# Four-layer decoder trunk on one core: sums of scaled x made in two parts and placed between the plain column tiles of each FFN

## The chip, the cores and the metric

The kernel runs on one core of a Trainium2 chip. The core's engines run side by side, each in the order of its own list of instructions, and wait for each other through semaphores: PE (TensorE) multiplies matrices, DVE (VectorE) and ACT (ScalarE) work element by element, POOL (GpSimd) and SP (SyncE) here mostly start transfers. The metric is device time in microseconds (us) of one execution; three runs of the kernel before took 1972.0 to 1973.74 us, median 1972.96 us. The profile is of a fourth execution.

## The reference, cut to what matters

Two layers; each is FFN, mixer, FFN. The mixer of layer 0 is differential attention, that of layer 1 a gated spatial MLP. x is 512 tokens by 1024 features in float32, an FFN's inner width is 2816.

```python
def _rmsnorm(x, g):
    y = xf * lax.rsqrt(jnp.mean(xf * xf, axis=-1, keepdims=True) + RMS_EPS)
    return (y * g.astype(jnp.float32)).astype(x.dtype)

def _swiglu_ffn(x, w_gate_up, w_down):
    g, u = jnp.split(x @ w_gate_up, 2, axis=-1)
    return (jax.nn.silu(g) * u) @ w_down

for i in range(DEPTH):
    x = x + 0.5 * _swiglu_ffn(_rmsnorm(x, ffn1_norm[i]), ffn1_w_gate_up[i], ffn1_w_down[i])
    # mixer: x = x + attention(_rmsnorm(x)) in layer 0, x + sgu(_rmsnorm(x)) in layer 1
    x = x + 0.5 * _swiglu_ffn(_rmsnorm(x, ffn2_norm[i]), ffn2_w_gate_up[i], ffn2_w_down[i])
```

## The kernel before, in words

**Layout.** x lies transposed in SBUF, eight tiles x[k] of 128 features by 512 tokens. Each fp32 operand of a product is split into a high part in a reduced format and the low rest (`hi`, `lo`; ACT copies the high part, DVE subtracts), and a product is three matmuls, hi·hi, hi·lo and lo·hi (`mm3`). So each weight piece of 128 by 1024 costs ACT a copy (`...h`) and DVE a subtraction (`...l`) before PE can use it (`split`, buffers in a ring of four).

**The four FFNs** are named f0 to f3 (f0 and f1 stand around the attention, f2 and f3 around the MLP; their norms are n0, n2, n3, n5). The 22 column tiles of gate and up form eleven pairs (j, j + 11). The first two pairs are made plainly: four *plain tiles*, 0, 11, 1, 12 in this order, of 48 matmuls 128x512 each: eight k, gate and up, three matmuls. Their weight pieces are called f1w{tile}{half}: f1w110 is the first half of tile 11, f1w11 the second half of tile 1. The other nine pairs are made in seven products instead of eight (names P1, P2, Q3, Q4, Q5, P6, P7), each for gate (a) and up (b): 14 *turns* of 12 matmuls 128x256, in the order P1a, P1b, Q5a, P6a, P6b, Q5b, P7a, P7b and so on. These products need sums and differences of weight pieces and seven *sums of scaled x* per kp = 0..3 (x[kp] and x[kp + 4] times the norm's gain and the row scale, with their halves added and subtracted). After the third, sixth and ninth pair, and at the end, `down_part` does a part of the down projection.

**The row scale.** The plain products use x times the gain only; the row scale 1/rms is multiplied in later. PE sums the squares (`Norm.rstd`, tile n2ss in f1), DVE makes the reciprocal root in some ten small steps (n2v, n2y, n2t), builds two diagonal tiles (n2dgh, n2dgl), PE spreads them over the partitions (`Norm.rows`, n2rb), ACT copies the result (n2rbs, `rb` in the code). In every FFN before, the sum of squares stands in the PE's list after k = 3 of a plain tile (the second tile in f0, the first in the others), the spreading after k = 7 of that tile.

**What `rb` lets go.** `gated` makes silu(gate)·up of a plain tile, `halves_of` splits it for the down projection, `scaled(kp)` makes the seven sums of one kp in one tile and splits them at once (f1x0h, f1x0l: 128x1792). In the program, `scaled` for all four kp is written after all four plain tiles, and P1a of the first pair (w2, tile f1w2Xa) needs all four.

**Order.** PE's order inside an FFN is the program's (`keep_in_program_order`). The lists of DVE and ACT are made by the tile framework's scheduler, which may move an instruction past others; once compiled the order is fixed.

Of the kernel before, what the change touches and what calls it, by code (L numbers as in the profile page):

```python
# [56 lines left out]
def kernel(  # L57
# [220 lines left out]
    def ffn(layer, which, norm, nxt):  # L278
# [10 lines left out]
        slot = {"P1": 0, "P2": 1, "Q4": 2, "Q5": 3, "P6": 4, "P7": 5, "Q3": 6}  # L289
        turns = ["P1a", "P1b", "Q5a", "P6a", "P6b", "Q5b", "P7a", "P7b", "P2a", "P2b", "Q3a", "Q3b", "Q4a", "Q4b"]  # L290

        with ExitStack() as c:
# [17 lines left out]
            xf, rb, late = [], None, []  # L310

            def gated(j, ps):
                h = room(f"{nm}r{j}")
                g, u = h[:, :2, :], h[:, 2:4, :]
# [4 lines left out]
                late_halves.append((j, u))  # L319

            def scaled(kp):

                h = room(f"{nm}x{kp}")
                for k, dst in ((kp, h[:, 0:8:7, :]), (kp + 4, h[:, 1:3, :])):
# [12 lines left out]
                xf.append((hi, lo))  # L337

            late_halves = []
            plain = [j for i in range(PLAIN) for j in (i, i + FH)]  # L340
            held = []
            for at, j in enumerate(plain):
                if first and at == 0:
                    parts = begin(norm)
                else:
                    parts = [
                        split(load(gate_up[f, j][:, q * D:(q + 1) * D], f"{nm}gu{j}{q}"), D, f"{nm}w{j}{q}")
                        for q in range(2)
                    ]
                ps = [bank(f"{nm}p{j}{u}", "ps" if first and at == 1 else "pp") for u in range(2)]  # L350
                for k in range(KT):
                    wh, wl = parts[k // 4]
                    for u in range(2):
                        c0 = slice((k % 4 * 2 + u) * P, (k % 4 * 2 + u + 1) * P)
# [1 line left out]
                    if rb is None and at == first:
                        if k == 3:
                            r = norm.rstd()
                        elif k == KT - 1:
                            rb = norm.rows(r)  # L360
                late.append((j, ps))
                if at == 1:
                    for unit in late:
                        gated(*unit)
                    late = []
            for kp in range(4):
                scaled(kp)
            for unit in late:
                gated(*unit)
            for unit in late_halves:  # L370
                halves_of(*unit)

            def gate_up_pair(i):
# [653 lines left out]
```

## Time and profile before

The profiled execution took 1971.33 us; its span, first to last instruction, is 1969.6 us.

| | busy us | share of the span | instructions |
|---|---|---|---|
| PE | 1935.8 | 98% | 11626 |
| PEld (weight loads of PE) | 1712.2 | 87% | 11626 |
| DVE | 1327.3 | 67% | 2127 |
| ACT | 879.0 | 45% | 1336 |
| POOL | 65.1 | 3% | 83 |

The mean granted clock of TensorE over the span is 0.992 of full speed. The chain that ended last is 92% PE, 6% DVE, 1% ACT and 1% issue. A share of busy time is a mean over the whole program; a busy matmul at half the clock counts as busy too. So the places where PE waits, and what it does right behind them, have to be read from the timeline.

### The profile page before, as it was taken

To read this page: it belongs to the slowest core of one execution; us is meant where nothing else is said; L and a number is where in the kernel's file an instruction comes from. 1 tells how busy PE (TensorE), PEld (TensorE's weight loads), DVE (VectorE), ACT (ScalarE), POOL (GpSimd) and SP (SyncE) were. 2 spreads that over 40 slices of the span, in tenths; PEclk is the share of its full clock that TensorE was granted. 3 is DMA by queue.
4 is the path that set the end of the run, shared out by engine and by line. 5 is a ranking of instruction groups with operands and counts; after the bars stand their busy time and mean duration, and the time that the engine had idled before them with its cause. 6 is when DMAs were issued, how large, how long until landed. Compare 5 with 4: busy or idle time off the path is not lost.

```text
span 1969.6 us, 29451 instructions
## 1 busy us (share of the span) xinstructions
PE 1935.8 (98%) x11626; PEld 1712.2 (87%) x11626; DVE 1327.3 (67%) x2127; ACT 879.0 (45%) x1336; POOL 65.1 (3%) x83
## 2 busy tenths in 40 slices
PE   8899999999999999999999999999999999999999
PEld 7889898877777799999879999988888887999997
DVE  8757574667878866666686666755595568666663
ACT  5535353555654444445445344533332234444451
POOL 0000000000000000000000000000000000000000
PEclk9899999999999999999999999999999999999999
DMA  6354552312112345454335546443333233454542
GB/s 206 97 141 133 140 136 89 129 64 70 55 54 86 83 131 148 131 140 131 112 82 137 130 138 150 124 140 116 105 116 97 86 107 86 133 144 132 139 124 80
DMA packets 89275, 228.58 MB, mean 116 GB/s; under 512 B 10033, under 2 KB 43185, under 8 KB 89137
## 3 DMA queue, kind: packets, MB, share of 16 engines
q1 hardware_dynamic: 78768, 188.95, 29.5%
q0 software_dynamic: 10368, 37.75, 11.5%
q8 instruction: 91, 1.49, 0.3%
q14 instruction: 48, 0.39, 0.1%
HBM read 224.56 MB, written 2.10 MB: 115 GB/s over the span
## 4 chain that ended last, share of the span: by engine, by line
PE 92%; DVE 6%; issue 1%; ACT 1%; DMA 0%; SPq 0%
PE f3dp L133 6%; PE f0dp L133 6%; PE f2dp L133 6%; PE f1dp L133 6%; PE gup L133 4%; PE gop L133 4%; PE aop L133 2%; PE v1p L133 1%; PE qk2p L133 1%; PE v0p L133 1%; PE qk1p L133 1%; PE qk0p L133 1%; PE gv0p L133 1%; PE gv1p L133 1%; PE gv2p L133 1%; PE gv3p L133 1%
## 5 line engine op out<-in xcount | busy, mean ns | idle before, releaser
L439 DVE SCALAR_TENSOR_TENSOR x<-f3dp,x 128x512 f32<-128x512 f32 x32 | 22.1, 691 | 60.2 <-PE f3dp L133 60.2
L439 DVE SCALAR_TENSOR_TENSOR x<-f0dp,x 128x512 f32<-128x512 f32 x32 | 22.1, 690 | 49.1 <-PE f0dp L133 49.1
L439 DVE SCALAR_TENSOR_TENSOR x<-f2dp,x 128x512 f32<-128x512 f32 x32 | 22.1, 690 | 49.1 <-PE f2dp L133 49.1
L439 DVE SCALAR_TENSOR_TENSOR x<-f1dp,x 128x512 f32<-128x512 f32 x32 | 22.1, 690 | 48.9 <-PE f1dp L133 48.9
L918 DVE TENSOR_TENSOR x<-gop,x 128x512 f32<-128x512 f32 x24 | 16.6, 690 | 20.0 <-PE gop L133 20.0
L898 ACT ACTIVATE gh<-gut 128x512 fp32r<-128x512 f32 x16 | 10.1, 633 | 42.6 <-DVE gut L897 42.6
L761 DVE TENSOR_TENSOR x<-aop,x 128x512 f32<-128x512 f32 x32 | 21.5, 685 | 1.9 <-PE aop L133 1.8
L888 PEld LDWEIGHTS gs<-wT,gv 128*128 128x128 f32 x128 | 16.1, 191 | 0.9
L893 DVE TENSOR_TENSOR gst<-gs,bs 128x512 f32<-128x512 f32 x16 | 11.0, 687 | 8.8 <-PE gs L888 8.8
L888 PE MATMUL gs<-wT,gv 128*128 128x128 f32 x128 | 16.2, 274 | 0.0
L838 ACT ACTIVATE gv<-gv 128x512 f32<-128x512 f32 x16 | 10.1, 629 | 12.4 <-DVE gv L837 12.3
L857 DVE TENSOR_TENSOR gut<-gup,n4rbs 128x512 f32<-128x512 f32 x16 | 10.9, 684 | 6.6 <-PE gup L133 6.6
L858 ACT ACTIVATE gut<-gut,sm 128x512 f32<-128x512 f32 x16 | 11.5, 721 | 6.7 <-DVE gut L857 6.5
L899 DVE TENSOR_TENSOR gl<-gut,gh 128x512 fp32r<-128x512 f32 x16 | 11.0, 686 | 4.2 <-ACT gh L898 4.2
L264 POOL DMA_DIRECT2D f1w2b<-in_gate_up_dram x1 | 0.9, 865 | 356.1 <-DVE f1w2t L260 356.1
L873 DVE SCALAR_TENSOR_TENSOR gv<-gv,lnmv,lng 128x512 f32<-128x512 f32 x16 | 11.5, 741 | 1.6 <-DMA lng<-in_ln_g_dram 1.6
L874 DVE SCALAR_TENSOR_TENSOR gv<-gv,lny,lnb 128x512 f32<-128x512 f32 x16 | 11.6, 746 | 1.1 <-DMA lnb<-in_ln_b_dram 1.1
L416 ACT ACTIVATE f1r<-f1r 128x512 f32<-128x512 f32 x9 | 5.7, 632 | 14.6 <-DVE f1r L414 14.6
L264 POOL DMA_DIRECT2D f3w2b<-in_gate_up_dram x1 | 0.9, 880 | 342.1 <-DVE f3w2t L260 342.1
L416 ACT ACTIVATE f0r<-f0r 128x512 f32<-128x512 f32 x9 | 5.7, 633 | 14.3 <-DVE f0r L414 14.3
L416 ACT ACTIVATE f3r<-f3r 128x512 f32<-128x512 f32 x9 | 5.7, 633 | 14.3 <-DVE f3r L414 14.3
L416 ACT ACTIVATE f2r<-f2r 128x512 f32<-128x512 f32 x9 | 5.7, 633 | 14.3 <-DVE f2r L414 14.3
(20869 smaller groups left out, 8068.0 us busy)
## 6 DMA issues: line engine op xcount, KB each, us to landing
f0d<-in_down_dram SPq DMA_DIRECT2D x48, 192.0 KB, 2.5
f1d<-in_down_dram SPq DMA_DIRECT2D x48, 192.0 KB, 2.5
f2d<-in_down_dram SPq DMA_DIRECT2D x48, 192.0 KB, 2.5
f3d<-in_down_dram SPq DMA_DIRECT2D x48, 192.0 KB, 2.5
f1gu<-in_gate_up_dram SPq DMA_DIRECT2D x8, 512.0 KB, 3.6
f2gu<-in_gate_up_dram SPq DMA_DIRECT2D x8, 512.0 KB, 3.6
f3gu<-in_gate_up_dram SPq DMA_DIRECT2D x8, 512.0 KB, 3.6
f0gu<-in_gate_up_dram SPq DMA_DIRECT2D x6, 512.0 KB, 4.8
```

Source lines behind the costliest of these rows:

```text
L133: mm = nc.tensor.matmul(ps, stationary, moving, start=start, stop=stop, skip_group_check=more)
L416: nc.scalar.activation(g[:, 2:, :], g[:, 2:, :], AF.Silu)
L439: nc.vector.scalar_tensor_tensor(x[m], pt, 0.5, x[m], op0=ALU.mult, op1=ALU.add)
L761: nc.vector.tensor_tensor(x[m], pt, x[m], op=ALU.add)
L857: nc.vector.tensor_tensor(ut, ps, rr["rb"], op=ALU.mult)
L858: nc.scalar.activation(ut, ut, AF.Gelu, bias=sm[:, C_BU + c:C_BU + c + 1])
L873: nc.vector.scalar_tensor_tensor(vv, vv, mv[:, n, 0:1], gr, op0=ALU.subtract, op1=ALU.mult)
L874: nc.vector.scalar_tensor_tensor(vv, vv, rr["y"][:, n:n + 1], lr, op0=ALU.mult, op1=ALU.add)
L888: nc.tensor.matmul(ps[:, n * P:(n + 1) * P], v32[n][:, c * P:(c + 1) * P], wT[:, g, :], start=True, stop=True)
L893: nc.vector.tensor_tensor(t.rearrange("p (n t) -> p n t", t=P), ps.rearrange("p (n t) -> p n t", t=P), bs[:, g, :].unsqueeze(1).broadcast_ ...
L899: nc.vector.tensor_tensor(gl, ut, f32(gh), op=ALU.subtract)
L918: nc.vector.tensor_tensor(x[m], pt, x[m], op=ALU.add)
```

## The change

Three things are changed, all at the head of an FFN.

First, `scaled(kp)` becomes `x_first(kp)` (step A: the two scalings, the first difference, a copy by ACT, and the split of four of the seven results, f1xa0h and f1xa0l, 128x1024) and `x_rest(kp)` (step B: the other three sums and their split, f1xb0h and f1xb0l, 128x768). P1, P2, Q4 and Q5 read the first part, Q3, P6 and P7 the second. A table of steps (A, B, `t`/`r` for gating a plain tile, `h` for its halves, product names for splits of the first pair's weights) says after which plain tile each is written. Second, f0 has three plain pairs instead of two, and so eight instead of nine made in seven products. Third, in f1 the sum of squares is taken after k = 5 instead of k = 3, and its spreading four k later, after k = 1 of the second tile; the first table entry then runs right behind the spreading.

```diff
-PLAIN = 2
+RSTD_AT = (3, 5, 3, 3)
+STEPS = ("A0 t0 h0 B0", "A1 t1 h1 B1", "P1 A2 t2 A3 Q5", "P6 B2 B3 r3 h2 h3")
+FIRST_STEPS = ("", "A0 t0 h0 B0", "A1 t1 h1 B1", "A2 B2", "P1 A3 B3 r2 r3 Q5", "P6 r4 r5 h2 h3 h4 h5")
...
+            plain = [j for i in range(3 if first else 2) for j in (i, i + FH)]
...
-                hi, lo = (
-                    fp.tile([P, 7, HT], F32R, tag="x" + q, name=f"{nm}x{kp}{q}", bufs=4) for q in "hl"
-                )
-                nc.scalar.activation(hi, h[:, :7, :], AF.Copy)
-                nc.vector.tensor_tensor(lo, h[:, :7, :], f32(hi), op=ALU.subtract)
+            def x_halves(kp, name, h, n):
+                hi, lo = (
+                    fp.tile([P, n, HT], F32R, tag=f"x{name}{q}", name=f"{nm}x{name}{kp}{q}", bufs=4) for q in "hl"
+                )
+                nc.scalar.activation(hi, h, AF.Copy)
+                nc.vector.tensor_tensor(lo, h, f32(hi), op=ALU.subtract)
+                return hi, lo
...
+            def x_first(kp):
+                h, h2 = scaled[kp] = room(f"{nm}x{kp}"), room(f"{nm}y{kp}")
+                for k, dst in ((kp, h2[:, 0:2, :]), (kp + 4, h[:, 1:3, :])):
                     nc.vector.scalar_tensor_tensor(
                         dst, two(x[k]), norm.gain(k), two(rb), op0=ALU.mult, op1=ALU.mult
                     )
+                nc.vector.tensor_tensor(h[:, 3, :], h2[:, 1, :], h[:, 2, :], op=ALU.subtract)
+                nc.scalar.activation(h[:, 0, :], h2[:, 0, :], AF.Copy)
+                xform[kp, 0] = x_halves(kp, "a", h, 4)
+
+            def x_rest(kp):
+                h, h2 = scaled.pop(kp)
+                nc.vector.tensor_tensor(h2[:, 2, :], h[:, 3, :], h2[:, 0, :], op=ALU.subtract)
+                nc.vector.tensor_tensor(h2[:, 3, :], h2[:, 0, :], h2[:, 1, :], op=ALU.subtract)
+                nc.vector.tensor_tensor(h2[:, 1, :], h[:, 1, :], h2[:, 2, :], op=ALU.add)
+                xform[kp, 1] = x_halves(kp, "b", h2[:, 1:, :], 3)
...
+                    when = at * KT + k - (KT if first else 0)
+                    if when == RSTD_AT[f]:
+                        found.append(norm.rstd())
+                    elif when == RSTD_AT[f] + 4:
+                        rb = norm.rows(found.pop())
+                        if delayed:
+                            run(delayed.pop())
...
+            parts = {0: begin(norm) if first else splits(0)}
+            parts[1] = splits(1)
+            for at in range(len(plain)):
+                products(at, parts.pop(at))
+                if at + 2 < len(plain):
+                    parts[at + 2] = splits(at + 2)
+                if rb is None:
+                    delayed.append(steps[at])
+                else:
+                    run(steps[at])
```

The result is three moves in the lists of the engines. In f1's list on PE the sum of squares stood behind k = 3 before:

```order
L133 MATMUL f1p_6427<-n2x3h,f1w00h 128x512
L133 MATMUL f1p_6427<-n2x3l,f1w00h 128x512
L133 MATMUL f1p_6427<-n2x3h,f1w00l 128x512
L133 MATMUL n2ss<-ones,n2acc 128x1 x4
L133 MATMUL f1p_6426<-n2x4h,f1w01h 128x512
L133 MATMUL f1p_6426<-n2x4l,f1w01h 128x512
```

and now:

```order
L135 MATMUL f1p_6367<-n2x5h,f1w01h 128x512
L135 MATMUL f1p_6367<-n2x5l,f1w01h 128x512
L135 MATMUL f1p_6367<-n2x5h,f1w01l 128x512
L135 MATMUL n2ss<-ones,n2acc 128x1 x4
L135 MATMUL f1p_6366<-n2x6h,f1w01h 128x512
L135 MATMUL f1p_6366<-n2x6l,f1w01h 128x512
```

Twelve matmuls (k = 4 and 5) have moved in front of n2ss. In f1's list on DVE, the end of the reciprocal root (n2y, n2t), the diagonal tiles and the weight half f1w11l stood like this before:

```order
L151 SCALAR_TENSOR_TENSOR n2t<-n2t,n2v 128x4
L152 SCALAR_TENSOR_TENSOR n2y<-n2t,n2y 128x4
L203 TENSOR_SCALAR n2rh<-n2y 128x4
L204 TENSOR_TENSOR n2rl<-n2y,n2rh 128x4
L208 TENSOR_TENSOR n2dgh<-ident,n2rh 128x512
L208 TENSOR_TENSOR n2dgl<-ident,n2rl 128x512
L126 TENSOR_TENSOR f1w11l<-f1gu_6586,f1w11h 128x1024
```

and now, with what follows (f1y and f1x are the scaled x, f1r the gated tile, f1xa0l the first part's low half, f1w120l a half of the fourth tile's weights):

```order
L153 SCALAR_TENSOR_TENSOR n2t<-n2t,n2v 128x4
L128 TENSOR_TENSOR f1w11l<-f1gu_6441,f1w11h 128x1024
L154 SCALAR_TENSOR_TENSOR n2y<-n2t,n2y 128x4
L205 TENSOR_SCALAR n2rh<-n2y 128x4
L206 TENSOR_TENSOR n2rl<-n2y,n2rh 128x4
L210 TENSOR_TENSOR n2dgh<-ident,n2rh 128x512
L210 TENSOR_TENSOR n2dgl<-ident,n2rl 128x512
L344 SCALAR_TENSOR_TENSOR f1y_6475<-x_77,sm,n2rbs 128x512
L344 SCALAR_TENSOR_TENSOR f1x_6474<-x_81,sm,n2rbs 128x512
L320 TENSOR_TENSOR f1r_6484<-f1p_6366,n2rbs 128x512
L347 TENSOR_TENSOR f1x_6474<-f1y_6475,f1x_6474 128x256
L322 TENSOR_TENSOR f1r_6484<-f1p_6367,n2rbs 128x512
```

f1w11l has moved in front of the last step of the root, and the scaling of x follows the diagonal tiles at once. Last, the end of the sums on DVE in f1. Before, the last low half of the sums, f1x3l, stood here, followed by f1h1l (half of a gated tile) and the gating of the fourth plain tile:

```order
L126 TENSOR_TENSOR f1w2P6l<-f1w2t,f1w2P6h 128x1024
L318 TENSOR_TENSOR f1r_6748<-f1r_6748 128x512
L336 TENSOR_TENSOR f1x3l<-f1x_6737,f1x3h 128x1792
L308 TENSOR_TENSOR f1h1l<-f1r_6748,f1h1h 128x512
L315 TENSOR_TENSOR f1r_6753<-f1p_6654,n2rbs 128x512
```

and now f1xa3l, which P1a needs, stands eleven places ahead of f1xb3l, which P6a needs:

```order
L334 TENSOR_TENSOR f1xa3l<-f1x_6654,f1xa3h 128x1024
L128 TENSOR_TENSOR f1w2P6l<-f1w2t,f1w2P6h 128x1024
L355 TENSOR_TENSOR f1y_6640<-f1y_6640 128x256
L354 TENSOR_TENSOR f1y_6655<-f1x_6654,f1y_6655 128x256
L356 TENSOR_TENSOR f1y_6640<-f1x_6639,f1y_6640 128x256
L355 TENSOR_TENSOR f1y_6655<-f1y_6655 128x256
L320 TENSOR_TENSOR f1r_6738<-f1p_6669,n2rbs 128x512
L334 TENSOR_TENSOR f1xb2l<-f1y_6640,f1xb2h 128x768
L356 TENSOR_TENSOR f1y_6655<-f1x_6654,f1y_6655 128x256
L322 TENSOR_TENSOR f1r_6738<-f1p_6670,n2rbs 128x512
L310 TENSOR_TENSOR f1h1l<-f1r_6649,f1h1h 128x512
L334 TENSOR_TENSOR f1xb3l<-f1y_6655,f1xb3h 128x768
```

So one wait for all seven sums has become two waits, one at P1a for four of them and one three turns later for the rest. Counted over the whole list of f1, 53 instructions stand on DVE from the first scaling (f1y) to f1xb3l. Attention and the gated MLP keep their lists.

## Rows read from the trace of the kernel before

**Rows 1.** PE's waits: engine line waited for: us in total, times, longest us
```profile
PE f1w2Xa L133 <- ACT f1x3h L335: 2.7, 1, 2.7
...
PE n2ss L133 <- DVE n2acc L188: 2.5, 1, 2.5
...
PE f1w2Xa L133 <- DVE f1x3l L336: 1.9, 1, 1.9
```
**Rows 2.** Timeline, PE, f1: start us, us, engine line op out<-in xcount
```profile
674.01 0.28 PE L133 MATMUL f1w2Xa<-f1x0h,f1w2P1h 128*128 128x256 f32 x1
...
685.50 0.28 PE L133 MATMUL f1w2Xa<-f1x0h,f1w2P6h 128*128 128x256 f32 x1
```
**Rows 3.** Timeline, PE, the same places of f0, f2 and f3
```profile
53.41 0.28 PE L133 MATMUL f0w2Xa<-f0x0h,f0w2P1h 128*128 128x256 f32 x1
...
68.24 0.29 PE L133 MATMUL f0w2Xa<-f0x0h,f0w2P6h 128*128 128x256 f32 x1
...
84.08 0.28 PE L133 MATMUL f0w3Xa<-f0x0h,f0w3P1h 128*128 128x256 f32 x1
...
1027.50 0.28 PE L133 MATMUL f2w2Xa<-f2x0h,f2w2P1h 128*128 128x256 f32 x1
...
1038.14 0.28 PE L133 MATMUL f2w2Xa<-f2x0h,f2w2P6h 128*128 128x256 f32 x1
...
1657.19 0.28 PE L133 MATMUL f3w2Xa<-f3x0h,f3w2P1h 128*128 128x256 f32 x1
...
1668.61 0.28 PE L133 MATMUL f3w2Xa<-f3x0h,f3w2P6h 128*128 128x256 f32 x1
```
**Rows 4.** Timeline, PE, around f1's sum of squares and row scale
```profile
629.99 0.39 PE L133 MATMUL f1p<-n2x3h,f1w00l 128*128 128x512 f32 x1
632.85 1.02 PE L133 MATMUL n2ss<-ones,n2acc 128*128 128x1 f32 x8 [2.47 <-DVE n2acc L188]
633.73 0.76 PE L133 MATMUL f1p<-n2x4h,f1w01h 128*128 128x512 f32 x1
...
640.88 0.39 PE L133 MATMUL n2rb<-n2dgh,ones_r 128*128 128x512 f32 x1
...
644.09 0.39 PE L133 MATMUL f1p<-n2x2h,f1w110h 128*128 128x512 f32 x1
```
**Rows 5.** Windows, f1: us, busy of PE PEld DVE ACT POOL, PEclk, DMA
```profile
681.00:685.00 4.00, 4.00 (x20) 4.00 (x20) 2.73 (x5) 2.42 (x5) 0.00 (x0) 0.51 0.62 118
```
**Rows 6.** Timeline, DVE, f1's reciprocal root and diagonal tiles
```profile
636.90 0.16 DVE L152 SCALAR_TENSOR_TENSOR n2y<-n2t,n2y 128x4 f32<-128x4 f32 x1
...
637.38 0.68 DVE L208 TENSOR_TENSOR n2dgh<-ident,n2rh 128x512 fp32r<-128x512 f32 x1
637.99 0.69 DVE L208 TENSOR_TENSOR n2dgl<-ident,n2rl 128x512 fp32r<-128x512 f32 x1
```
**Rows 7.** Timeline, ACT, f1, a weight half and the row scale
```profile
640.86 1.06 ACT L125 ACTIVATE f1w11h<-f1gu 128x1024 fp32r<-128x1024 f32 x1 [9.05 <-PE f1p L133]
641.82 0.58 ACT L216 ACTIVATE n2rbs<-n2rb 128x512 f32<-128x512 f32 x1
```
**Rows 8.** Timeline, DVE, f1, first sums of scaled x
```profile
651.77 0.69 DVE L315 TENSOR_TENSOR f1r<-f1p,n2rbs 128x512 f32<-128x512 f32 x1 [1.96 <-PE f1p L133]
652.38 0.74 DVE L325 SCALAR_TENSOR_TENSOR f1x<-x,sm,n2rbs 128x512 f32<-128x512 f32 x1
...
658.64 0.75 DVE L325 SCALAR_TENSOR_TENSOR f1x<-x,sm,n2rbs 128x512 f32<-128x512 f32 x1
659.30 0.42 DVE L330 TENSOR_TENSOR f1x<-f1x 128x256 f32<-128x256 f32 x1
659.64 0.42 DVE L328 TENSOR_TENSOR f1x<-f1x 128x256 f32<-128x256 f32 x1
659.98 1.22 DVE L126 TENSOR_TENSOR f1w2P1l<-f1w2a,f1w2P1h 128x1024 fp32r<-128x1024 f32 x1
661.11 2.02 DVE L336 TENSOR_TENSOR f1x0l<-f1x,f1x0h 128x1792 fp32r<-128x1792 f32 x1
```

More of the change, by code (lines that the diff above doesn't have):

```diff
@@ L294, in ffn, with room @@
             fp = c.enter_context(tc.tile_pool(name=nm + "p", bufs=1, reuse_waits="tile"))
-            def room(name):
-                return fp.tile([P, 8, HT], F32, tag="room", name=name, bufs=2)
+            def room(name, tag="room"):
+                return fp.tile([P, 4, HT], F32, tag=tag, name=name, bufs={"room": 4, "t": 2}[tag])
             def two(t):
@@ L308, in halves_of, with gated @@
                 nc.vector.tensor_tensor(two(lo), u, f32(two(hi)), op=ALU.subtract)
[L310 to L314, printed above, removed]
+            ready, gates, rb = {}, {}, None
+            plain = [j for i in range(3 if first else 2) for j in (i, i + FH)]
+            def gated(at, tag):
+                j, ps = plain[at], ready.pop(at)
+                h = room(f"{nm}r{j}", tag)
+                g, u = h[:, :2, :], h[:, 2:, :]
                 nc.vector.tensor_tensor(g, two(ps[0]), two(rb), op=ALU.mult)
@@ L318, in gated, with halved @@
                 nc.vector.tensor_tensor(u, u, g, op=ALU.mult)
[L319 to L324, printed above, removed]
+                gates[at] = u
+            def halved(at):
+                halves_of(plain[at], gates.pop(at))
+            def x_halves(kp, name, h, n):
[5 more added lines that the diff above has]
+                return hi, lo
+            scaled, sums, xform = {}, {}, {}
+            def x_first(kp):
+                h, h2 = scaled[kp] = room(f"{nm}x{kp}"), room(f"{nm}y{kp}")
+                for k, dst in ((kp, h2[:, 0:2, :]), (kp + 4, h[:, 1:3, :])):
                     nc.vector.scalar_tensor_tensor(
@@ L335, in scaled @@
-                nc.scalar.activation(hi, h[:, :7, :], AF.Copy)
-                nc.vector.tensor_tensor(lo, h[:, :7, :], f32(hi), op=ALU.subtract)
[L337 to L350, printed above, removed]
+                nc.vector.tensor_tensor(h[:, 3, :], h2[:, 1, :], h[:, 2, :], op=ALU.subtract)
@@ new lines, in splits, with products @@
+            def splits(at):
+                j = plain[at]
+                return [
+                    split(load(gate_up[f, j][:, q * D:(q + 1) * D], f"{nm}gu{j}{q}"), D, f"{nm}w{j}{q}")
+                    for q in range(2)
+                ]
+            def products(at, parts):
+                nonlocal rb
+                j = plain[at]
+                tags = (("pp", "pp"), ("pp", "pp"), ("ps", "ps"), ("pp", "pp"), ("pp", "pp"), ("ps", "po"))[at]
+                ps = ready[at] = [bank(f"{nm}p{j}{u}", tags[u]) for u in range(2)]
@@ L355, in ffn, with weigh_of @@
                         mm3(ps[u], wh[:, c0], wl[:, c0], norm.xh[k], norm.xl[k], k == 0, k == KT - 1)
[L356 to L373, printed above, removed]
+                    when = at * KT + k - (KT if first else 0)
[5 more added lines that the diff above has]
+                            run(delayed.pop())
+            def weigh_of(i):
                 quarter = lambda j, q: gate_up[f, j][:, q * D:(q + 1) * D]
-                weigh = Weigh(
+                return Weigh(
                     fp, {"a": quarter(i, 0), "b": quarter(i + FH, 0), "c": quarter(i + FH, 1), "d": quarter(i, 1)},
@@ L378, in gate_up_pair, with take, run @@
                 )
-                h = room(f"{nm}r{i}")
-                g, h = h[:, :4, :], h[:, 4:, :]
+            found, delayed = [], []
+            weighs = {}
+            start = plain[-2] + 1
+            def take(prod):
+                if prod == "P1":
+                    weighs[start] = weigh_of(start)
+                weighs[start].take(prod)
+            def run(names):
+                for step in names.split():
+                    what, n = step[0], step[1:]
+                    if what == "A":
+                        x_first(int(n))
+                    elif what == "B":
+                        x_rest(int(n))
+                    elif what == "t":
+                        gated(int(n), "t")
+                    elif what == "r":
+                        gated(int(n), "room")
+                    elif what == "h":
+                        halved(int(n))
+                    else:
+                        take(step)
+            steps = FIRST_STEPS if first else STEPS
+            parts = {0: begin(norm) if first else splits(0)}
[6 more added lines that the diff above has]
+                    delayed.append(steps[at])
+                else:
+                    run(steps[at])
+            def gate_up_pair(i):
+                weigh = weighs.pop(i) if i in weighs else weigh_of(i)
+                g, h = room(f"{nm}g{i}"), room(f"{nm}r{i}")
                 keep, acc = {}, {}
@@ L444, in down_part @@
                             nc.sync.dma_start(out[m], x[m])
-            for i in range(PLAIN, FH):
+            for i in range(start, FH):
                 gate_up_pair(i)
```

11 lines of the change are left out of this document (4 added, 7 removed).

## The prediction

> **What bounds the kernel now.** I read the page first: PE is busy nearly throughout, so only its gaps and its slow stretches can be won. The list of PE's waits says where the gaps are. In f1 its first product of the first pair, f1w2Xa, waits 2.7 us for ACT's last high half of the sums of scaled x and then 1.9 us for DVE's last low half, and the sum of squares n2ss waits 2.5 us for DVE [rows 1]. f2 and f3 show the same two waits for sums, f0 four of them. Then I read PE's timeline there, by starts, since a start cannot be modelled away. A plain matmul takes 0.2267 us: from 644.09 to P1a's first at 674.01 there are 132 (six k and two tiles) in 29.92 us [rows 2, 4]. A turn takes 1.44 us: f0's eleven turns from P6a to the next pair need 84.08 - 68.24 = 15.84 us [rows 3]. By this rate P6a starts three turns, 4.32 us, behind P1a; what is more is lost. Last come the windows: behind f1's waits the granted clock is 0.51, the 1.2 GHz level, for the four microseconds in which P1b and most of Q5a run [rows 5]. So a wait costs itself and then a slow stretch, and both are in the difference of starts.
>
> **The change part by part.** The sum is made against the profiled execution, 1971.33 us (1.63 below the median of 1972.96).
>
> *P1a's wait in f1, f2, f3.* P6a starts 685.50 - 674.01 = 11.49 us behind P1a in f1, 10.64 in f2 and 11.42 in f3 [rows 2, 3]. Less 4.32 this is 7.17, 6.32 and 7.10 us lost, 20.59 together. It ends if DVE has the first parts (A0 to A3) by P1a and the second parts by P6a's last k. Is that so? DVE's prices, from start to start: 0.66 for a scaling 128x512, 0.34 for 128x256, 1.13 for 128x1024 [rows 8], 0.61 for 128x512 [rows 6]; 128x768 was not there before, between the last two, 0.87. From f1's first scaling to f1xb3l the list holds 53: 8 scalings (5.28), 16 of 128x256 (5.44), 14 of 128x512 (8.54), 11 of 128x1024 (12.43) and 4 of 128x768 (3.48), in all 35.2 us if DVE never waits. When it starts comes below.
>
> *f1's later sum of squares.* Before, k = 3 ends at 629.99 + 0.23 = 630.22, n2ss can start at 632.85, and k = 2 of the second tile starts at 644.09; the 24 matmuls behind n2ss take 640.88 - 633.73 = 7.15 us [rows 4], against 24 x 0.2267 = 5.44. Now k = 4 and 5 (2.72 us) run first, so n2ss comes at 632.94, when the squares are there, and its own 0.88 us [rows 4] ends at 633.82. Four more k (5.44) bring PE to the spreading, n2rb, at 639.26. But DVE is not ready. Its last root step could be at 636.90 - 632.85 = 4.05 us behind n2ss [rows 4, 6], 636.99, were f1w11l not in front of it now. f1w11l needs ACT's f1w11h, which waits for a buffer that PE frees with the first tile's last matmul, 633.82 + 2.72 = 636.54; 1.06 us on ACT [rows 7] and 1.13 on DVE make it 638.75. From the last root step to the end of the second diagonal tile it is 637.99 + 0.69 - 636.90 = 1.78 us [rows 6], so n2rb's second matmul starts at 640.5 and k = 2 at 640.75. That is 3.34 us sooner than 644.09, with a new wait of about 1.0 us.
>
> That rests on DVE not passing a waiting instruction. The row shows it: the gating f1r (L315) idled 1.96 us for PE, and the scaling listed behind it, whose scale ACT had made by 642.4, started only after it [rows 7, 8]. The Trainium skill says the same (page "PSUM — Partial Sum Buffer", section "Engine vs sequencer instructions"): the queues of ScalarE, VectorE and GpSimdE are strict FIFO. By this rule f1's wait stands; could DVE pass f1w11l, 1.0 us more would be won.
>
> *Does f1's cover suffice?* From k = 2 at 640.75 PE has 29.92 us to P1a, 670.67; P6a follows at 674.99, and its tenth matmul, the first with kp = 3, 1.1 us later; the low half is due at 676.2. DVE's first scaling waits for n2rb (0.39 behind 640.5 [rows 4]) and its copy, 0.58 [rows 7], so 641.5; with 35.2 us f1xb3l is ready at 676.7. A wait of 0.5 us is left at P6a. f1xa3l is eleven places earlier (6.4 us by these prices), at 670.3, and in time. Queued behind f1xb3l are the gate of the fourth tile and P7's split, due three turns later: no loss. In f2 and f3 the spreading is where it was, so PE has 2.72 us more to do behind it, and f1h1l (0.61) stands behind the sums there; f1w11l's like (1.13) is ahead. 0.5 - 2.72 - 0.61 + 1.13 leaves 1.7 us to spare: no wait.
>
> *f0.* P1a starts at 53.41 now. One more plain pair, 96 x 0.2267 = 21.76 us, takes it to 75.17. The first pair in seven products then begins with w3, which before started at 84.08 [rows 3]: 8.91 us won. This counts P1a's whole loss, 68.24 - 53.41 - 4.32 = 10.51, less the price of the plain pair, 21.76 - 14 x 1.44 = 1.60. f0's sums have 21.8 us more cover than elsewhere. Its queue of loads carries four more plain pieces early and w2's four no more; the splits ahead of them free their places two plain tiles (21.8 us) before they are needed.
>
> *At nothing:* ACT's four copies of 128x256 per FFN and eight more copies of halves lie on an engine that is idle more than half of the time; their cost shows only if DVE waits behind them. The cover is thin in f1 alone. Unknown is how much DVE idles there for ACT: below by 0; above I take the 1.96 us of rows 8. Each microsecond there costs one. Below nothing: f1's two waits (1.5 us) could be missing.
>
> Sum: 20.59 + 3.34 - 0.5 + 8.91 = 32.3 us. 1971.33 - 32.3 = 1939.0, and on the median, 1972.96 - 32.3 = **1940.7 us**.
>
> **The rivals.**
> *Short waits drop the clock in f1.* The waits of 1.0 us at n2rb and 0.5 at P6a are new places where the clock may fall to the 1.2 GHz level, as it did behind 2.5 and 4.6 us. Price: 7.15 - 5.44 = 1.7 at the first, and 7.17 - 2.7 - 1.9 = 2.6 at the second, 1945. For it: both are waits of PE in a full stretch. Against: both are shorter than any behind which I read a fall. The Trainium skill bears on it (page "TensorE: Matmul & The Clock Gate", section "A second HAM failure mode: psum-queue depth-cycling"): frequent short idles also made a clock swing between its levels. By that the time would be the 1945 just given; no run here shows it.
>
> *The wait only moves.* The sums are in the list where the change says, but halves wait on ACT behind weight copies that wait for PE's buffers, and DVE idles between. If that is 4 us in each of f1, f2 and f3, PE waits at P6a 4.0, 2.3 and 2.3 us more, with a slow stretch of 2.6 us behind each: 16.4 us back, 1957. For it: f1w120h now stands ahead of f1xa0h on ACT. Against: going down both lists with the durations above I find a buffer free within half a microsecond of ACT's coming to it.
>
> *Slower.* One mechanism: the splits of the last plain tile (f1w121l and its likes) stand behind sums, and if they come late PE waits at k = 4 of that tile. It is due at 640.75 + 36 x 0.2267 + 48 x 0.2267 + 24 x 0.2267 = 665.2. In f1 the list puts f1w121l fifteenth from the first scaling: 3 scalings, 4 of 128x256, 4 of 128x512, one of 128x768 and 3 of 128x1024, 10.0 us, at 651.5. From 13.7 us later on PE waits; to lose the 32.3 us, 8.1 in each FFN, it must be 21.8 us later. Time then above 1973. Nothing in the profile points to it.
>
> *No change within 0.2%* (3.9 us, about what a measurement of this kernel can tell): the sums stay together, or something later gives all of it back; the order of f1 on DVE speaks against the first, the unchanged lists of attention and MLP against the second.
>
> **How the numbers follow.** The forecast 0.72, clock in f1 0.12, the wait moved 0.12, slower 0.02, no change 0.02. The first three are faster by over 0.2%: 0.96; same 0.02; slower 0.02. Range: down by f1's two waits, 1.5 us, and 2 us for what runs differ (the three shown spread 1.74), to 1937; up over the first rival (1945), DVE's idle time at its upper bound (1.96 us in f1 and, past the 1.7 to spare, 0.3 in f2 and in f3), and 1.5 us between runs, to 1949. The moved wait is mostly left out.
>
> **What would show it.** Right: PE's waits list no sums of scaled x at P1a; P6a starts 4.3 us behind P1a in f2 and f3 and under 5 in f1; w3 of f0 starts near 75.2; n2ss waits for nothing, n2rb about 1 us for n2dgl; the clock is 1.00 behind each of these. Wrong: P6a waits over 1 us in f2 or f3 (DVE's total or ACT's part), a granted clock near 0.5 behind n2rb, or a plain tile that waits for its weight halves.

## The result, and the profile after

The changed kernel takes 1939.62 us (median of four runs, 1939.39 to 1939.77); the kernel before took 1972.8 beside it. The ratio is 0.9832, 95% interval 0.9814 to 0.9849. The forecast was 1940.7. The profiled execution took 1939.39 us, its span 1937.7, 31.9 less than before, where the forecast's sum was 32.3. The mean granted clock is 1.000 (0.992 before). By the medians the gain is 33.2 us: the profiled execution of the kernel before, 1971.33, lies below all four beside the result. The time is 1.1 below the forecast although the profiled gain is 0.4 short of the sum; with a spread of 1.7 us in the kernel before, so near a fit of the medians is partly luck, and the two profiles are what tests the sum. One execution of the kernel before, beside a later run, took 2703.88 us at a mean clock of 0.657 and is left out of every comparison.

PE's waits in the kernel after (who waited for whom, us in total, times, longest):

```profile
PE f0p L135 <- ACT w00wh L239: 5.1, 1, 5.1
PE n2rb L135 <- DVE n2dgh L210: 0.6, 1, 0.6
PE f1w2Xa L135 <- DVE f1xb3l L334: 0.6, 1, 0.6
...
PE a4s L710 <- ACT a4e L729: 0.4, 1, 0.4
```

Against [rows 1]: the waits for sums of scaled x at P1a are gone in all four FFNs, and so is that of n2ss. The two new ones stand in f1, where the forecast put them; the long one of f0 is the start of the program.

PE's timeline after, the places of [rows 2 to 4] (start, us, engine, line, operation):

```profile
75.28 0.28 PE L135 MATMUL f0w3Xa<-f0xa0h,f0w3P1h 128*128 128x256 f32 x1
...
623.80 0.39 PE L135 MATMUL f1p<-n2x5h,f1w01l 128*128 128x512 f32 x1
624.03 0.95 PE L135 MATMUL n2ss<-ones,n2acc 128*128 128x1 f32 x8
...
630.14 0.39 PE L135 MATMUL f1p<-n2x1h,f1w110l 128*128 128x512 f32 x1
631.16 0.47 PE L135 MATMUL n2rb<-n2dgh,ones_r 128*128 128x512 f32 x1 [0.63 <-DVE n2dgh L210]
631.67 0.50 PE L135 MATMUL n2rb<-n2dgl,ones_r 128*128 128x512 f32 x1
632.01 0.39 PE L135 MATMUL f1p<-n2x2h,f1w110h 128*128 128x512 f32 x1
...
661.95 0.28 PE L135 MATMUL f1w2Xa<-f1xa0h,f1w2P1h 128*128 128x256 f32 x1
...
666.27 0.28 PE L135 MATMUL f1w2Xa<-f1xb0h,f1w2P6h 128*128 128x256 f32 x1
...
667.34 0.31 PE L135 MATMUL f1w2Xa<-f1xb3h,f1w2P6h 128*128 128x256 f32 x1
668.27 0.39 PE L135 MATMUL f1w2Xa<-f1xb3l,f1w2P6h 128*128 128x256 f32 x1 [0.61 <-DVE f1xb3l L334]
668.49 0.28 PE L135 MATMUL f1w2Xa<-f1xb3h,f1w2P6l 128*128 128x256 f32 x1
...
1008.99 0.28 PE L135 MATMUL f2w2Xa<-f2xa0h,f2w2P1h 128*128 128x256 f32 x1
...
1013.30 0.28 PE L135 MATMUL f2w2Xa<-f2xb0h,f2w2P6h 128*128 128x256 f32 x1
...
1632.35 0.28 PE L135 MATMUL f3w2Xa<-f3xa0h,f3w2P1h 128*128 128x256 f32 x1
...
1636.66 0.28 PE L135 MATMUL f3w2Xa<-f3xb0h,f3w2P6h 128*128 128x256 f32 x1
```

In f1, f2 and f3 P6a now starts 4.31 to 4.32 us behind P1a, three turns, where it was 10.6 to 11.5. The row at 630.14 ends at 630.37 by the matmul's rate; without a wait the two n2rb (0.45 us) would let k = 2 start at 630.82, so n2rb's wait costs 1.2.

The granted clock behind the two new waits (windows of after: us, busy time of PE, PEld, DVE, ACT and POOL, clock, DMA share and GB/s):

```profile
633.00:635.00 2.00, 2.00 (x11) 1.65 (x10) 2.00 (x4) 0.69 (x2) 0.00 (x0) 1.00 0.02 6
...
669.00:671.00 2.00, 2.00 (x19) 2.00 (x18) 2.00 (x3) 1.54 (x3) 0.00 (x0) 1.00 0.14 14
```

It is 1.00, the 2.4 GHz level, behind both. Last, DVE in f1 (timeline of after; in brackets idle time before the row and its end):

```profile
628.71 1.23 DVE L128 TENSOR_TENSOR f1w11l<-f1gu,f1w11h 128x1024 fp32r<-128x1024 f32 x1 [0.74 <-ACT f1w11h L127]
629.86 0.15 DVE L154 SCALAR_TENSOR_TENSOR n2y<-n2t,n2y 128x4 f32<-128x4 f32 x1
...
632.84 0.75 DVE L344 SCALAR_TENSOR_TENSOR f1y<-x,sm,n2rbs 128x512 f32<-128x512 f32 x1 [1.22 <-ACT n2rbs L218]
...
667.25 0.96 DVE L334 TENSOR_TENSOR f1xb3l<-f1y,f1xb3h 128x768 fp32r<-128x768 f32 x1
```

f1w11l stands and waits ahead of the last root step. From the first scaling to f1xb3l DVE shows no idle time: 667.25 + 0.87 - 632.84 = 35.28 us; the forecast added up 35.2.

### The profile page after: what moved, and what is told of

The parts are those of the page before. It is cut to its first block, busy times and chain, and to the rows that moved or that the text cites. A ratio compares the mean times of both kernels' runs of the same rounds, so it can differ in the third digit from the quotient of the medians.

```text
span 1937.7 us, 29348 instructions
## 1 busy us (share of the span) xinstructions
PE 1926.3 (99%) x11554; PEld 1701.1 (88%) x11554; DVE 1321.8 (68%) x2135; ACT 879.4 (45%) x1358; POOL 63.2 (3%) x81
## 4 chain that ended last, share of the span: by engine, by line
PE 96%; DVE 3%; issue 0%; ACT 0%; DMA 0%; SPq 0%; ACTq 0%
PE f3dp L135 6%; PE f2dp L135 6%; PE f1dp L135 6%; PE f0dp L135 6%; PE gup L135 5%; PE gop L135 4%; PE f0p L135 3%; PE aop L135 2%; PE f3p L135 2%; PE f2p L135 2%; PE v1p L135 1%; PE v0p L135 1%; PE qk1p L135 1%; PE qk0p L135 1%; PE gv0p L135 1%; PE gv1p L135 1%
## 5 line engine op out<-in xcount | busy, mean ns | idle before, releaser
L909 ACT ACTIVATE gut<-gut,sm 128x512 f32<-128x512 f32 x16 | 11.5, 721 | 5.7 <-DVE gut L908 5.6
L924 DVE SCALAR_TENSOR_TENSOR gv<-gv,lnmv,lng 128x512 f32<-128x512 f32 x16 | 11.5, 742 | 1.2 <-DMA lng<-in_ln_g_dram 1.2
L467 ACT ACTIVATE f1g<-f1g 128x512 f32<-128x512 f32 x9 | 5.7, 633 | 14.3 <-DVE f1g L465 14.3
L467 ACT ACTIVATE f2g<-f2g 128x512 f32<-128x512 f32 x9 | 5.7, 633 | 14.3 <-DVE f2g L465 14.3
L467 ACT ACTIVATE f3g<-f3g 128x512 f32<-128x512 f32 x9 | 5.7, 633 | 14.3 <-DVE f3g L465 14.3
L948 DVE TENSOR_TENSOR gut<-gut,gst 128x512 f32<-128x512 f32 x16 | 11.0, 689 | 1.1 <-DVE gst L944 0.5
```

What stands on the lines that cost most here:

```text
L467: nc.scalar.activation(g[:, 2:, :], g[:, 2:, :], AF.Silu)
L909: nc.scalar.activation(ut, ut, AF.Gelu, bias=sm[:, C_BU + c:C_BU + c + 1])
L924: nc.vector.scalar_tensor_tensor(vv, vv, mv[:, n, 0:1], gr, op0=ALU.subtract, op1=ALU.mult)
L948: nc.vector.tensor_tensor(ut, ut, t, op=ALU.mult)
```

## The experiments

My theory was the prediction's: DVE begins the sums early enough, the two parts have two deadlines three turns apart, f0 needs the third pair as cover, and what is left in f1 is DVE's total. The rivals were that the place in the program alone does it, that the third pair alone does it, and that short waits drop the clock. Times of one group are to be compared with each other: the kernel before took 1972.32 us beside the first four, 1972.77 beside the next four. Three parts of the change were not named where it was described, and the runs bear on them: the gated tiles of the steps `t` have two buffers of their own, `room` has four buffers of half the size instead of two, and the plain tiles use other PSUM banks (the third tile `ps` instead of `pp`, so that by the program's order the fifth of f0 follows the second).

**f0 with two plain pairs.**

```diff
-            plain = [j for i in range(3 if first else 2) for j in (i, i + FH)]
-FIRST_STEPS = ("", "A0 t0 h0 B0", "A1 t1 h1 B1", "A2 B2", "P1 A3 B3 r2 r3 Q5", "P6 r4 r5 h2 h3 h4 h5")
+            plain = [j for i in range(2) for j in (i, i + FH)]
+FIRST_STEPS = ("", "A0 t0 h0 B0 A1 t1 h1 B1", "P1 A2 t2 A3 Q5", "P6 B2 B3 r3 h2 h3")
```

> The changed kernel with two plain pairs in f0 again instead of three; the sums in two parts and their places stay. My theory (f0 needs the third pair as cover): DVE begins the scalings at 33.5 us and needs about 33 us for its list to f0xb3l, so P1a of w2 at 53.5 waits some 5.7 us for the last first part and P6a 1 to 2 us for the last second part, with a slow stretch of about 2.6 us behind; less the 1.60 us that the plain pair costs, the time rises by 6 to 9 us, to 1946 to 1949 us. Rival (the placing and the two parts alone are enough in f0): PE does not wait, and the time falls by the 1.60 us of the pair, to 1938 us.

Measured: 1946.27 us (1946.04 to 1946.82), ratio to before 0.9869 (0.9854 to 0.9883). PE's waits in this kernel:

```profile
PE f0w2Xa L135 <- ACT f0xa3h L333: 2.8, 1, 2.8
PE f0w2Xa L135 <- DVE f0xa3l L334: 0.9, 1, 0.9
PE f0w2Xa L135 <- DVE f0xa2l L334: 0.8, 1, 0.8
...
PE f0w2Xa L135 <- DVE f0xb3l L334: 0.4, 1, 0.4
```

From 60 to 64 us the clock is 0.50. So placing and parts alone do not do it in f0. In this profile w3 starts at 82.7, 1.4 us sooner than before where the changed kernel gains 8.8: 7.4 us hang on the third pair by the starts, 6.7 by the medians.

**The third pair alone**, in the kernel before:

```diff
-PLAIN = 2
+PLAIN = (3, 2, 2, 2)
...
-            plain = [j for i in range(PLAIN) for j in (i, i + FH)]
+            plain = [j for i in range(PLAIN[f]) for j in (i, i + FH)]
```

> The kernel before with three plain pairs in f0 and nothing else. My theory (the third pair pays only together with the placing): P1a of f0 finds its sums ready, but the fifth plain tile needs the banks of the third, whose gating now stands behind three of the four sums on DVE, at about 60 us where the tile is due at 53.5: a wait of about 7 us and a slow stretch there, and the pair's price of 1.60; 1970 to 1975 us. Rival (cover is all that f0 lacked): 8.9 us faster than before, 1964 us.

Measured: 1970.76 us, ratio 0.9994 (0.9984 to 1.0003). In f0, PE's fifth plain tile and the gating on DVE for which it waits:

```profile
59.77 0.77 PE L133 MATMUL f0p<-n0x0h,f0w20h 128*128 128x512 f32 x1 [6.28 <-DVE f0r L315]
```

```profile
58.94 0.68 DVE L315 TENSOR_TENSOR f0r<-f0p,n0rbs 128x512 f32<-128x512 f32 x1
```

The sums are in time for P1a, but the gating that frees a bank stands behind them on DVE. Neither half of f0's change gains much without the other (w3 starts 0.8 us sooner here). What the rest of the change has to bring for it is not shown: this kernel lacks the order of the steps, and also the other banks, by which the fifth tile needs the gating of the second tile and not of the third.

**f1's sum of squares at k = 3 again** (`RSTD_AT = (3, 3, 3, 3)`).

> The changed kernel with f1's sum of squares behind k = 3 again, the spreading four k later. My theory: n2ss waits about 2.5 us for DVE's squares as in the kernel before and a slow stretch follows, P1a of f1 starts 3.3 us later than in the changed kernel; the wait of 0.9 us at P6a goes, since the sums have 2.7 us more cover: 2.4 us slower, 1942.0 us (1941.3 to 1943.0). Rival (the later sum of squares is worth nothing, since DVE's last sum sets the end of this stretch either way): 1939.6 us, with PE waiting less somewhere behind.

Measured: 1941.01 us, four runs from 1940.07 to 1942.96; ratio 0.9842 (0.9825 to 0.9858). The profiled run took 1941.85; n2ss waits 2.5 us, nothing waits at P6a, and P1a to w3 takes 20.2 us. Behind n2ss the clock was low in this run (windows of this kernel):

```profile
626.00:630.00 4.00, 4.00 (x14) 3.14 (x14) 3.62 (x15) 0.00 (x0) 0.00 (x0) 0.71 0.81 252
```

The profiled run agrees with my theory (2.4 us of span). But two runs took 1940.1 at a mean clock of 1.000. They were not profiled, but by their clock and time it did not fall in them behind this wait; in all four profiles that have the wait of 2.5 us (this one, the kernel before, the third pair alone, buffers alone) it did. Where it holds, the later sum of squares is worth 0.5 us (2.5 us waited instead of 1.2 and 0.9); where it falls, 2.3 and more.

**Buffers alone.** The kernel before, with only this:

```diff
+            def gate_room(name):
+                return fp.tile([P, 4, HT], F32, tag="t", name=name, bufs=2)
...
-                h = room(f"{nm}r{j}")
-                g, u = h[:, :2, :], h[:, 2:4, :]
+                h = gate_room(f"{nm}r{j}")
+                g, u = h[:, :2, :], h[:, 2:, :]
```

> The kernel before with one edit: the gated plain tiles get buffers of their own, so the sums of scaled x no longer wait for the gating of the second tile to free theirs; the sums stay in one piece and are written behind the plain tiles. Theory A (the sums began too late for lack of a buffer, and the scheduler places them early as soon as it can): PE's waits for sums at P1a go, but the splits for Q5 and P6 now stand behind the sums, and some 2 to 4 us per FFN come back at Q5a or P6a: 1957 to 1967 us. Theory B (one piece can't be ready by P1a, the two parts with their two deadlines are what counts): the waits for sums at P1a stay, and the time is within 3 us of the kernel before, 1970 to 1975 us.

Measured: 1968.62 us, ratio 0.9983 (0.9973 to 0.9992): between the two. In f2, DVE makes the last sums before P1a (1027.8), in f1 and f3 4.8 us before it; but the splits of the first pair's weights come behind:

```profile
1024.30 2.02 DVE L339 TENSOR_TENSOR f2x3l<-f2x,f2x3h 128x1792 fp32r<-128x1792 f32 x1 [0.62 <-ACT f2x3h L338]
...
1030.44 1.22 DVE L126 TENSOR_TENSOR f2w2Q5l<-f2w2t,f2w2Q5h 128x1024 fp32r<-128x1024 f32 x1
...
1034.52 1.23 DVE L126 TENSOR_TENSOR f2w2P6l<-f2w2t,f2w2P6h 128x1024 fp32r<-128x1024 f32 x1
```

and PE waits for these instead (its timeline, f2):

```profile
1031.71 0.39 PE L133 MATMUL f2w2Ya<-f2x0h,f2w2Q5l 128*128 128x256 f32 x1 [0.66 <-DVE f2w2Q5l L126]
1034.54 0.38 PE L133 MATMUL f2w2Xa<-f2x0h,f2w2P6h 128*128 128x256 f32 x1 [1.37 <-ACT f2w2P6h L125]
1035.80 0.38 PE L133 MATMUL f2w2Xa<-f2x0h,f2w2P6l 128*128 128x256 f32 x1 [0.76 <-DVE f2w2P6l L126]
```

From 1037 to 1041 the clock is 0.63. P1a to w3 takes 25.2 us, before 26.5, after 20.2. Theory A had the mechanism (the sums began late for lack of a buffer, and the splits are late next) but priced the new waits too low: it left out the slow stretch behind them, and f0, where PE now waits 5.8 us for P1's split and w3 starts 2.7 us later than before. So sums in one piece can be ready by P1a in f1, f2 and f3, and theory B is wrong; what the two parts add to the buffers, if the splits too were placed early, is not shown, since no kernel with sums in one piece, buffers of their own and early splits was run.

**The steps written late**, in two parts and with their buffers:

```diff
-STEPS = ("A0 t0 h0 B0", "A1 t1 h1 B1", "P1 A2 t2 A3 Q5", "P6 B2 B3 r3 h2 h3")
+STEPS = ("t0 h0", "t1 h1", "P1 t2", "A0 A1 B0 A2 B1 A3 Q5 P6 B2 B3 r3 h2 h3")
```

> The changed kernel with all eight steps A and B of f1, f2 and f3 written behind the last plain tile, as the kernel before had its sums; f0 is as in the changed kernel. Theory A (the place in the program decides little here: DVE's list is made by the scheduler, which moves a step forward as soon as its inputs and a buffer are there; what counts is that the sums are in two parts with buffers of their own): P1a of f2 and f3 waits for nothing, P6a under 1 us, and the time is within 3 us of the changed kernel, 1939 to 1943 us. Theory B (the place in the program is what brings the sums forward): P1a waits for them again, about 20 us back over the three FFNs, 1955 to 1962 us.

Measured: 1940.43 us (1940.19 to 1940.68), ratio 0.9837 (0.9823 to 0.9850). The changed kernel itself, run beside it:

> The changed kernel as it is, once more, as the measure for the three that are sent with it: 1939.6 us (1939.2 to 1940.5).

Measured: 1939.44 us (1939.29 to 1939.94). Of the sums only these waits show in the late version:

```profile
PE f1w2Xa L135 <- DVE f1xb3l L334: 0.6, 1, 0.6
...
PE f1w2Xa L135 <- DVE f1xa3l L334: 0.4, 1, 0.4
```

Theory A holds: in f1, f2 and f3 the place of the steps A and B in the program is worth 1.0 us of some 23 (31.9 less f0's 8.8). The scheduler brings them forward by itself; the parts and the buffers together let it. For f0, whose steps stay in their places here, it is not shown.

**f1w11l behind the diagonal tiles.** DVE is made to keep this order in f1:

```diff
+        if name == "f1w11":
+            tc.keep_in_program_order(low)
...
+                if self.name == "n2":
+                    tc.keep_in_program_order(dgi)
...
+                if f == 1 and at == 1:
+                    parts[2] += splits(2, (1,))
                 if at + 2 < len(plain):
-                    parts[at + 2] = splits(at + 2)
+                    parts[at + 2] = splits(at + 2, (0,) if f == 1 and at == 0 else (0, 1))
```

> The changed kernel with f1w11l put behind the second diagonal tile n2dgl in f1's list on DVE (its split is written behind the spreading, and these two keep the program's order). My theory (DVE doesn't pass a waiting instruction, so n2rb's wait comes from f1w11l alone, and what DVE has to do up to f1xb3l is the limit): the last root step starts some 1.9 us sooner, n2rb waits for nothing, f1's first scaling starts 1.0 us sooner or more, but f1w11l's 1.13 us now lie behind it, so f1xb3l ends only some 0.5 us sooner, PE's wait at P6a grows from 0.6 to about 1.1 us, and 0.5 us of the time are won: 1939.1 us. Rival (the wait at n2rb has another cause, ACT or the buffers): n2rb still waits 0.6 us, and the time is the same.

Measured: 1938.71 us (1938.36 to 1939.41), the fastest of all kernels here; ratio to before 0.9829 (0.9815 to 0.9842). It is 0.7 us below the changed kernel beside it; one of its four runs lies among that kernel's. DVE in this kernel:

```profile
629.14 0.69 DVE L212 TENSOR_TENSOR n2dgl<-ident,n2rl 128x512 fp32r<-128x512 f32 x1
...
631.72 0.75 DVE L348 SCALAR_TENSOR_TENSOR f1y<-x,sm,n2rbs 128x512 f32<-128x512 f32 x1 [1.89 <-ACT n2rbs L222]
```

and what is left of PE's waits in f1:

```profile
666.64 0.38 PE L137 MATMUL f1w2Xa<-f1xb2l,f1w2P6h 128*128 128x256 f32 x1 [0.49 <-DVE f1xb2l L338]
667.50 0.38 PE L137 MATMUL f1w2Xa<-f1xb3l,f1w2P6h 128*128 128x256 f32 x1 [0.25 <-DVE f1xb3l L338]
```

n2rb waits for nothing, so f1w11l alone made that wait. f1's first scaling is 1.1 us sooner, but P6a still waits, 0.7 us in two places, and behind it PE is 0.8 sooner: a third of the gain is taken back by DVE's total, where half was expected. It is less because the scheduler also moved f1h1l (0.60 us) behind f1xb3l, which was not foreseen.

**Three halves on POOL.**

```diff
+        low = nc.gpsimd if name in ("f1w11", "f1w120", "f1w121") else nc.vector
-        nc.vector.tensor_tensor(wl[:, :n], raw[:, :n], f32(wh[:, :n]), op=ALU.subtract)
+        low.tensor_tensor(wl[:, :n], raw[:, :n], f32(wh[:, :n]), op=ALU.subtract)
```

> The changed kernel with three low halves of f1's plain weights (f1w11l, f1w120l, f1w121l) subtracted by POOL instead of DVE: DVE has 3.4 us less to do before f1xb3l. My theory (DVE's total is what is short in f1): n2rb's wait of 1.0 us and P6a's of 0.9 both go, 1.9 us faster than the changed kernel, 1937.7 us. Rival (POOL is slow at this, and its halves come late or take DVE's time): with more than 4 us for each half a plain tile waits for its weights or DVE's instructions beside it grow longer, and the time is 1939.6 us or more.

Measured: 1941.02 us (1940.58 to 1941.37), 1.6 slower than the changed kernel; ratio 0.9839 (0.9826 to 0.9853). My forecast failed, and the rival's second half is what happened. POOL and DVE in this kernel:

```profile
629.43 2.63 POOL L129 TENSOR_TENSOR f1w11l<-f1gu,f1w11h 128x1024 fp32r<-128x1024 f32 x1 [345.19 <-ACT f1w11h L127]
636.85 2.88 POOL L129 TENSOR_TENSOR f1w120l<-f1gu,f1w120h 128x1024 fp32r<-128x1024 f32 x1 [4.78 <-DVE f1r L323]
```

```profile
629.14 0.69 DVE L211 TENSOR_TENSOR n2dgh<-ident,n2rh 128x512 fp32r<-128x512 f32 x1
629.74 2.88 DVE L211 TENSOR_TENSOR n2dgl<-ident,n2rl 128x512 fp32r<-128x512 f32 x1
...
637.38 2.89 DVE L345 SCALAR_TENSOR_TENSOR f1y<-x,sm,n2rbs 128x512 f32<-128x512 f32 x1
...
646.00 2.19 DVE L335 TENSOR_TENSOR f1xa1l<-f1x,f1xa1h 128x1024 fp32r<-128x1024 f32 x1
```

A DVE instruction of 0.69 us that begins beside one of POOL's takes 2.88 and ends just behind it. The 2.2 us fall on n2dgl, for which PE then waits 1.2 us. From the first scaling to f1xb3l DVE again takes 35.4 us: two of the three halves (2.3 us) are gone from there, but f1y takes 2.1 us more and f1xa1l, beside POOL's third half (2.41 us from 644.70), 1.0 more. At P6a PE waits 1.5 us, not for a sum but for a copy by ACT:

```profile
668.94 0.39 PE L136 MATMUL f1w2Xa<-f1xb0h,f1w2P6h 128*128 128x256 f32 x1 [1.54 <-ACT f1k2a L456]
```

This copy, which reads the bank of P1a before P6a writes it, stands on ACT behind f1xb3h, and f1xb3h waited 0.85 us for DVE's late sums.

**The spreading sooner: waits of chosen length.**

```diff
+ROWS_AFTER = (4, 3, 2, 1)
...
-                    elif when == RSTD_AT[f] + 4:
+                    elif when == RSTD_AT[f] + ROWS_AFTER[f]:
```

> The changed kernel with the spreading of the row scale put sooner in PE's list: three k behind the sum of squares in f1, two in f2, one in f3, instead of four. DVE's list does not change, so PE must wait there: about 2.0 us in f1 (instead of 0.6), 1.5 us in f2, 2.85 us in f3. Theory A (a wait must have some length before the granted clock falls behind it; 0.6 and 0.9 us did not do it, 2.5 us in the kernel before did): the clock is 1.00 behind f2's wait and about 0.5 behind f3's, f1's in between. Theory B (what counts is the stretch around it, not the length): the clock falls behind none or all three. Price: 1.4 us in f1 less the 0.9 us that P6a's wait then spares, 1.5 in f2, 2.85 in f3: 4.9 us, and 1.7 us for each slow stretch: 1944.5 to 1949.6 us.

> As the one before, with the places changed round: two k behind the sum of squares in f1, one in f2, three in f3. Waits of about 3.3 us in f1, 2.85 us in f2 and 0.2 us in f3. Theory A: the clock is about 0.5 behind the first two and 1.00 behind the third. Theory B: as above, the same FFN keeps its clock whatever the length. 1.8 us in f1, 2.85 in f2, 0.2 in f3: 4.9 us, and 1.7 us for each slow stretch: 1944.5 to 1947.9 us.

Measured: 1946.50 us in one run of the first; its waits are 2.0, 1.5 and 2.8 us in f1, f2 and f3. With (4, 2, 1, 3): 1950.06 us in one run, above the 1947.9 expected at most; the waits are 3.4 in f1 and 2.8 in f2, and the clock was 0.50 behind both, from 634 to 636 and from 978.7 to 984. From w3 of f1 to P1a of f2 this kernel takes 6.0 us longer than the changed one, so the slow stretch in f2 cost some 3.2 us and not 1.7. The lengths came as forecast. The clock of this run fits theory A, that of the first kernel neither (0.50 behind 2.0 us in f1, 1.00 behind 2.8 us in f3), so the first kernel ran again:

> The kernel with f1's, f2's and f3's spreading three, two and one k behind the sum of squares, once more and with several runs, since in its first profile the clock fell behind the wait of 2.0 us in f1 and not behind the one of 2.8 us in f3, which neither length nor place explains. Theory C (whether the clock falls behind a wait of 2 to 3 us is open from run to run): the runs lie in steps of about 1.7 us between 1944.5 and 1949.6 us with mean clocks from 1.000 to 0.997, and the new profile need not show the fall at the same place. Theory D (it is fixed by the program): all runs within 0.5 us of 1946.5, and the clock falls in f1 alone again.

Measured: 1946.66 us (1946.53 to 1947.44), ratio 0.9870 (0.9852 to 0.9887), the same waits. Windows behind f1's and f3's wait in the first profile of this kernel:

```profile
632.00:634.00 2.00, 2.00 (x6) 1.57 (x5) 1.09 (x2) 0.90 (x2) 0.00 (x0) 0.50 0.32 125
...
1601.80:1603.00 1.20, 1.11 (x4) 0.73 (x5) 0.50 (x1) 0.10 (x1) 0.00 (x0) 1.00 0.47 191
```

and in the second:

```profile
632.00:634.00 2.00, 2.00 (x10) 1.67 (x9) 1.18 (x2) 0.99 (x2) 0.00 (x0) 1.00 0.39 150
...
1601.80:1603.00 1.20, 1.20 (x5) 0.91 (x3) 0.34 (x1) 0.60 (x1) 0.00 (x0) 0.50 0.06 14
```

The same program with the same waits, and the fall has moved from f1 to f3. So neither the length of a wait of 2 to 3 us nor its place decides alone: it is open from run to run (theory C), though the times here lay closer together than C said. What decides stays open.

**More work on DVE in f2 and f3.**

```diff
-                nc.vector.tensor_tensor(lo, h, f32(hi), op=ALU.subtract)
+                for again in range({"f2xb3": 2, "f3xb3": 5}.get(f"{nm}x{name}{kp}", 1)):
+                    nc.vector.tensor_tensor(lo, h, f32(hi), op=ALU.subtract)
```

> The changed kernel with the subtraction of the last low half repeated on DVE: once more in f2 (f2xb3l, 0.87 us more), four times more in f3 (3.48 us more). My theory (DVE has 1.75 us to spare in f2 and f3 between the end of this half and PE's use of it, and PE's wait at P6a is just what goes beyond): PE waits for nothing in f2, 1.7 us at P6a in f3, and 1941.3 us if the clock holds behind it, up to 1943.9 with a slow stretch. Rival (the list has slack elsewhere, or none): waits in both, 0.9 and 3.5 us, 1944 us or more, or none in either, 1939.6 us.

Measured: 1945.56 us in one run. f2 waits for nothing, as my theory said; f3 waits 4.5 us, not 1.7, the clock is 0.50 from 1643 to 1645, and w3 of f3 starts 6.2 us later than in the changed kernel (1658.7 for 1652.5). DVE's rows in f3 show why it waits so long:

```profile
1635.04 0.95 DVE L335 TENSOR_TENSOR f3xb3l<-f3y,f3xb3h 128x768 fp32r<-128x768 f32 x1
...
1640.33 1.21 DVE L128 TENSOR_TENSOR f3w2P7l<-f3w2b,f3w2P7h 128x1024 fp32r<-128x1024 f32 x1
1641.46 0.95 DVE L335 TENSOR_TENSOR f3xb3l<-f3y,f3xb3h 128x768 fp32r<-128x768 f32 x1
```

Between the repeats the scheduler put four other instructions (0.61, 0.60, 0.60 and 1.13 us, 2.94). 3.48 + 2.94 - 1.75 = 4.7, near the 4.5 listed: the time to spare was right, the list was not the one I assumed.

## Why the prediction was right, point by point

The gain can be read from the places where PE starts, before [rows 2 to 4] and after; w3 of f1, f2 and f3 stands at 701.34, 1053.98 and 1684.45 before and 683.01, 1029.14 and 1652.51 after.

| step | forecast | measured |
|---|---|---|
| f0 to w3 | 8.91 | 84.08 - 75.28 = 8.80 |
| f1 up to P1a | 3.34 | 674.01 - 661.95 - 8.80 = 3.26 |
| f1, P1a to w3 | 7.17 - 0.5 = 6.67 | 27.33 - 21.06 = 6.27 |
| f2, P1a to w3 | 6.32 | 26.48 - 20.15 = 6.33 |
| f3, P1a to w3 | 7.10 | 27.26 - 20.16 = 7.10 |
| all between these places | 0 | 0.2 |

- *The waits at P1a* went as priced. What the prediction did not say is why the sums came late: in the kernel before they lacked a buffer (buffers alone: the waits for sums at P1a go), and in f1, f2 and f3 the scheduler, not the place in the program, moves them (steps written late: 1.0 us). That they had to be in two parts is not shown.
- *The slow stretch behind a wait.* f2 and f3 show what the starts alone gave: the wait and the slow stretch behind it, 6.3 and 7.1 us for 4.6 and 4.5 us of waits listed.
- *f1.* The wait at n2rb was there and came from f1w11l, as forecast; it cost 1.2 where 1.0 was said. P6a's wait cost 0.9 where 0.5 was said: DVE's list took 35.28 for 35.2, its first scaling came 0.83 behind k = 2 for 0.75, and PE's restart took some 0.25: DVE goes on to its next row at 668.13, PE restarts at 668.27, and its next matmul follows after 0.22 instead of 0.12. This is the mis-sized term, 0.4 us: the prediction put the restart behind a wait at nothing.
- *The rival of short waits.* Its 1945 did not come: the clock is 1.00 behind both waits, and the mean clock is 1.000 in all eight runs of the changed kernel. The Trainium skill (page "TensorE: Matmul & The Clock Gate", section "A second HAM failure mode: psum-queue depth-cycling") speaks of frequent short idles; two of 0.6 us in a span of 1938 are few, and no run here tests the rule. My argument against it, that both waits are shorter than any with a fall behind it, was weaker than it looked, since above 2 us length did not decide either.
- *The wait that only moves* did not come: f2 and f3 wait for nothing at P6a. Where the weights' splits are not placed with the steps, it does come (buffers alone), though there it is the splits that are late and not the halves of the sums on ACT.
- *f0.* Cover of 21.8 us was enough with room: f0xb3l ends at 65.8 and is needed at 80.8 (the eleventh matmul of P6a, which starts at 79.59). Without the third pair 6.7 to 7.4 us are lost.

## What to carry to other kernels

Price a wait from the starts of the instructions around it, not from the wait listed: a slow stretch may lie behind it. Before crediting the place of a step in the program, look at the order that the scheduler made and at the buffers that bound it; a step freed without the steps that follow it in the same queue leaves the wait one place further on. Where an engine's list is full up to a deadline, moving one instruction within it gives part of the gain back (0.35 of 1.1 us here); taking work off it pays only if the engine that gets the work does not hold the first one up.
